# Weights of a hybrid decoder layer, laid out in DRAM by tiles

## The chip, the core and the metric

The kernel runs on one core of one Trainium2 chip. A core has a matrix engine (PE; its weight loads are shown apart as PEld), a vector engine (DVE), a scalar engine (ACT), a general engine (POOL) and a sync engine (SP) that here issues nearly all DMAs. Sixteen DMA engines move data between DRAM and the on-chip memory of 128 partitions. The metric is the device time of one execution in microseconds (us), the median of several runs. What the host does with the arrays before the launch is not part of it.

## The reference

One decoder layer on 512 tokens of width 2048, all in float32. A conditioning vector gives six modulation vectors. Then come two parallel groups of eight heads (HGRN2 and Gated DeltaNet), an output projection, and an MLP with squared ReLU.

```python
mod = c_act @ w_ada[l] + b_ada[l]                      # 2048 x 12288
sh_m, sc_m, gt_m, sh_f, sc_f, gt_f = jnp.split(mod[:, None, :], N_MOD, axis=-1)
h = rmsnorm(x, pre_mix_norm[l]) * (1.0 + sc_m) + sh_m
proj = h @ w_in[l]                                     # 2048 x 8208
o_hg = hgrn2_group(proj[..., :HG_COLS], lb_all[l], hg_norm[l])
o_gdn = gdn_group(proj[..., HG_COLS:], gdn_conv_w[l], gdn_a_log[l], gdn_dt_bias[l], gdn_norm[l])
y = jnp.concatenate([o_hg, o_gdn], axis=-1) @ w_out[l] # 2048 x 2048
x = x + gt_m * rmsnorm(y, post_mix_norm[l])
h = rmsnorm(x, pre_ffn_norm[l]) * (1.0 + sc_f) + sh_f
y = jnp.square(jax.nn.relu(h @ w_ff1[l])) @ w_ff2[l]   # 2048 x 8192, 8192 x 2048
x = x + gt_f * rmsnorm(y, post_ffn_norm[l])
```

## The kernel before

Every weight is read once; the profile counts 340 MB read from DRAM. A float32 product is made of three products of a narrower type: a matrix `a` is split into a high part `aH` and a low part `aL = a - aH`, and `mm3` adds aH·bH, aH·bL and aL·bH in PSUM.

**The weight stream.** All tiles of w_in, w_out, w_ff1 and w_ff2 go through `WeightStream` in an order fixed by `plan`. `_load` issues the DMA of a tile of 128 partitions by 1024 numbers (512 KB) into a `raw` buffer (three of them, six in the MLP), `_split` has ACT cast it to `wh` (L152) and DVE (for a few tiles of the start POOL) subtract it to `wl` (L154), and `get` hands both to PE and keeps loads up to three tiles ahead. In the MLP some w_ff2 tiles are first added or subtracted by POOL (L120).

**The start (about 0 to 200 us).** Shift and scale of the first modulation come from two segments of w_ada. `ada_slot` loads them in 128 tiles `adas` of 256 KB; ACT, DVE and POOL multiply them by the conditioning vector and add them up, PE sums over partitions, and the result modulates x block by block into `hH` and `hL`. As soon as a block of h is there, PE multiplies it with the first 32 tiles of w_in (`start_units`, heads 0 and 1). Such a tile joins two or four k-blocks of four or two column blocks of 128.

**The heads (about 200 to 1120 us).** PE runs the projections of heads 2 to 7 (`project`, tile `pj`: eight column blocks a head, each of two tiles of eight k-blocks, 96 tiles `in1`) between the recursions of the heads before. Beside them the other segments of w_ada are summed: `ada_rest` loads 192 tiles `ada` of 256 KB, 32 for each of these heads, at a pace set by `on_get`; ACT scales a tile, POOL adds it. After that come the output projection (40 tiles), the norms, and from about 1345 us the MLP (256 tiles, and 64 `ada` tiles of the last segment).

**What sets the order.** PE and SP run in the order in which the program writes their instructions, ACT too in the start; in the start and the heads the program interleaves threads by a running estimate of PE's time (`clock`) and of the loads' arrival (`on_load`). DVE and POOL, and ACT later, are ordered by the scheduler of the framework. All loads go out on SP's one queue, in order, so SP can stand at a buffer that isn't free while later loads wait behind it.

**How a tile was cut out.** In DRAM the weights have their reference layout, a row of w_in being 8208 numbers (32,832 bytes). The views below give a partition p the rows p, p+128 and so on, 128 to 512 columns each, so one partition's part of a tile is several short pieces. For w_ada, partition p takes rows 16p to 16p+15; one row is 49,152 bytes, so neighbouring partitions are 786,432 bytes apart.

```python
def w128(W, col, hf):
    return W[hf * 1024 : (hf + 1) * 1024, col : col + 128].rearrange("(k p) n -> p k n", p=P)
def wrow(W, r, nb):
    return W[r : r + 256, nb * 512 : (nb + 1) * 512].rearrange("(k p) n -> p k n", p=P)
```

Of the kernel before, what the change touches and what calls it, by code (L numbers as in the profile page):

```python
# [15 lines left out]
P = 128  # L16
# [18 lines left out]
D = 2048  # L35
# [5 lines left out]
GDN0 = 4096  # L41
C_HQ, C_HF, C_HI, C_HG = 0, 1024, 2048, 3072
C_GQ, C_GK, C_GV, C_GG, C_AB = 4096, 5120, 6144, 7168, 8192


class WeightStream:
# [41 lines left out]
    def _load(self):  # L88
        key, ap = self.loads[self.nl]
        raw = self._raw(key)  # L90
        aps = ap if isinstance(ap, list) else [ap]
        n = 1024 // len(aps)
        for j, a in enumerate(aps):
            self.nc.sync.dma_start(
                out=raw[:, j * n : (j + 1) * n].rearrange("p (k n) -> p k n", k=a.shape[1]), in_=a)
# [27 lines left out]
    def _split(self):  # L123
        i = self.ns
        e = self.plan[i]
        pool, nb = self.pool, self.bufs
        two = e[0][0] == "s2"
        if two and i not in self.raw:
            key = e[2][0]
            raw = self.raw[key]  # L130
        else:
            key = i
            raw = self.raw.pop(i)
            if two and len(e) > 3:
                key = e[2][0]
        self.uses[key] -= 1
        hn = ln = None
        if not two and len(e) > 2:
            if isinstance(self.alt, list):
                h, lo = self.alt.pop(0)  # L140
                hn = True
            else:
                pool, nb = self.alt, (0, e[2], e[2])
        if hn is None:
            tags = ("wh", "wl")
            if self.wide is not None and (two or len(e) == 2):
# [5 lines left out]
        self.cast = self.nc.scalar.copy(out=h, in_=raw).ins  # L152
        eng = self.nc.gpsimd if i in self.pool_l else self.nc.vector
        eng.tensor_tensor(out=lo, in0=raw, in1=h.bitcast(F32), op=ALU.subtract)  # L154
        ap = e[1]
        k = 2 if two else 8 if isinstance(ap, list) else ap.shape[1]
        self.hl[i] = (
            h.rearrange("p (k n) -> p k n", k=k),
            lo.rearrange("p (k n) -> p k n", k=k),
        )  # L160
        self.ns += 1
# [30 lines left out]
def hybrid_layer_kernel(  # L192
# [8 lines left out]
    PSUM = bass.MemoryType.PSUM  # L201
    xf = x[0]
    outf = out[0]
    Wi, Wo, W1, W2 = w_in[0], w_out[0], w_ff1[0], w_ff2[0]
    Wa = w_ada[0].rearrange("(p r) n -> p r n", p=P)

    const = ctx.enter_context(tc.tile_pool(name="const", bufs=1))
    big = ctx.enter_context(tc.tile_pool(name="big", bufs=1))
# [1 line left out]
    dram = ctx.enter_context(tc.tile_pool(name="dram", bufs=1, space=bass.MemoryType.DRAM))  # L210


    def w256(W, col, q):
        return W[q * 512 : (q + 1) * 512, col : col + 256].rearrange("(k p) n -> p k n", p=P)

    def wcols(W, cols, k0, nk):
        v = W[k0 * P : (k0 + nk) * P, :].rearrange("(k p) n -> p k n", p=P)
        return [v[:, :, cc : cc + P] for cc in cols]

    def w128(W, col, hf):  # L220
        return W[hf * 1024 : (hf + 1) * 1024, col : col + 128].rearrange("(k p) n -> p k n", p=P)

    def wrow(W, r, nb):
        return W[r : r + 256, nb * 512 : (nb + 1) * 512].rearrange("(k p) n -> p k n", p=P)


    G0, G1, H0, H1 = ([(k, h, cc) for cc in ccs] for k, h, ccs in (
        ("g", 0, (C_GQ, C_GK, C_GV, C_GG)), ("g", 1, (C_GQ, C_GK, C_GV, C_GG)),
        ("h", 0, (C_HF, C_HQ, C_HI, C_HG)), ("h", 1, (C_HF, C_HQ, C_HI, C_HG))))
    start_blocks = G0 + H0 + G1 + H1  # L230
    cuts = [(0, 2, 0, 16), (2, 2, 0, 16), (4, 2, 0, 8), (6, 2, 0, 8), (4, 4, 8, 16),
            (8, 4, 0, 8), (12, 4, 0, 8), (8, 4, 8, 16), (12, 4, 8, 16)]
    start_units = []
    for k0, nk, lo, hi in cuts:
        start_units += [(k0, nk, start_blocks[i : i + 8 // nk]) for i in range(lo, hi, 8 // nk)]
    NB_FF = DFF // P
    RB = 4
    NR = NB_FF // RB
    plan = []
    for i, (k0, nk, bls) in enumerate(start_units):  # L240
        plan.append((("in", i), wcols(Wi, [cc + h * P for _, h, cc in bls], k0, nk)))

    def plan_in1(col):
        for hf in range(2):
            plan.append((("in1", col, hf), w128(Wi, col, hf)))


    OUT_PAIRS = [8, 0, 10, 2, 12, 4, 14, 6]

    SLOT = dict(zip([r + i for r in OUT_PAIRS for i in (0, 1)], [i for i in range(16) if i % 4] + [0, 4, 8, 12]))  # L250

    for h in range(2, NH):
        for cc in (C_GK, C_GQ, C_GV, C_HF, C_HQ, C_HI, C_GG, C_HG):
            plan_in1(cc + h * P)
    for nbs in ((0,), (0, 1), (2,), (3,)):
        for i, r in enumerate(OUT_PAIRS):
            for nb in nbs:
                e = (("out", r, nb), wrow(Wo, r * P, nb))
                other = (nb == 3 and i >= 8 - NLAST) or (nb == 0 and len(nbs) == 2 and i > 0)
                plan.append(e + (NLAST,) if other else e)  # L260

    def plan_f2(r):
        for nb in range(4):
            for hf in range(RB // 2):
                e = (("f2", r, nb, hf), wrow(W2, r * RB * P + hf * 256, nb))
                plan.append(e + (2,) if r == NR - 1 and nb == 2 else e)


# [5 lines left out]
    def plan_s2(r, m):  # L274
        seen = set()
        for i, qa, op, qb in SEVEN:
            loads = []
            for q in (qa, qb):
                if q is not None and q not in seen:
                    seen.add(q)  # L280
                    loads.append(((r, m, q), wrow(W2, r * RB * P + (int(q[0]) - 1) * 256, m + 2 * (int(q[1]) - 1))))
# [10 lines left out]
    for kind, r, g in ff_order():  # L292
        if kind == 1:
            for q in range(4):
                plan.append((("f1", r * RB * P + g * 256, q), w256(W1, r * RB * P + g * 256, q)))
        else:
            plan_s2(r, g)
    plan_f2(NR - 1)
# [106 lines left out]
    def ada_load(alloc, col, ncol, r0, nr):  # L405
        a = alloc(f"ada{col}_{r0}")
        nc.sync.dma_start(out=a.rearrange("p (r n) -> p r n", r=nr), in_=Wa[:, r0 : r0 + nr, col : col + ncol])
        return a

    def ada_vector(a, ncol, r0, nr, acc, first):  # L410
# [138 lines left out]

    def late_loads():  # L550
        nc.sync.dma_start(out=cvr, in_=gdn_conv_w[0].rearrange("j (b n) -> (j b) n", n=P))
        nc.sync.dma_start(out=abraw, in_=Wi[:, C_AB : C_AB + 16].rearrange("(k p) n -> p k n", p=P))
# [694 lines left out]
    def ada_rest():  # L1247
# [275 lines left out]
    with ExitStack() as st:  # L1523
# [3 lines left out]
        def ada_gtf():  # L1527
# [251 lines left out]
```

## Time and profile before

| what | value |
|---|---|
| median of 3 runs | 2676.01 us (2669.79 to 2677.83) |
| the profiled execution: time, span | 2674.57 us, 2672.8 us |
| mean granted clock of PE | 0.974 |
| DMA packets | 335942, 350.66 MB, 131 GB/s on average |
| packets under 512 B, under 2 KB | 17191, 255001 |
| loads: w_in, ada, adas (median us to landing) | 10.9 (512 KB), 8.5, 5.4 (256 KB) |
| loads: w_out, w_ff (512 KB) | 3.8, 4.2 |

A view by windows has for each engine its busy time in a stretch and in brackets its instructions; then the granted clock of PE (1.00 is full speed), the mean busy share of the 16 DMA engines and the GB/s that they moved. A row of waits reads: engine, what it ran next and its line, what it had waited for, the sum in us, how often, the longest. L307 is the helper through which nearly all matmuls are recorded, so the tile's name tells them apart: `pj` projections of the heads, `pout` output projection, `pf` and `pg` the MLP.

### The profile page before, as it was taken

How to read it: one execution, taken by the hardware profiler on the slowest of the kernel's cores; microseconds unless marked ns; L12 is line 12 of the kernel's file. 1: busy time of each engine (PE TensorE's matmuls, PEld its weight loads, DVE VectorE, ACT ScalarE, POOL GpSimd, SP SyncE). 2: the span in 40 equal slices, each digit the busy share in tenths (PEclk: the TensorE clock that was granted, in tenths of full speed). 3: DMA queues.
4: the chain of work that ended last, by engine and by line, in shares of the span. 5: the costliest groups of instructions: out<-in, count | busy, mean ns of one | idle time of the engine just before them, and what ended most of it. 6: DMA issues, size and time to landing. Idle time of an engine off the chain costs nothing.

```text
span 2672.8 us, 34309 instructions
## 1 busy us (share of the span) xinstructions
PE 2497.4 (93%) x12627; PEld 2020.5 (76%) x12627; DVE 1870.6 (70%) x2709; ACT 1119.4 (42%) x1765; POOL 1036.3 (39%) x646
## 2 busy tenths in 40 slices
PE   5889999998996779999999999999999999999998
PEld 3667777787775567788778888888888888888876
DVE  7997868766764538553647668777778676777796
ACT  5543544444443324332444344444444444443333
POOL 5560344544543324000123554444544545533323
PEclk9999999999998889999999999999999999999999
DMA  9974886677889997452433334244243333332334
GB/s 289 279 192 72 133 123 138 140 151 144 146 129 100 87 117 105 91 172 95 160 115 130 111 124 136 95 135 137 96 138 129 104 130 117 106 117 86 112 103 165
DMA packets 335942, 350.66 MB, mean 131 GB/s; under 512 B 17191, under 2 KB 255001, under 8 KB 334621
## 3 DMA queue, kind: packets, MB, share of 16 engines
q1 hardware_dynamic: 335578, 348.42, 54.2%
q8 instruction: 99, 1.62, 0.2%
q14 instruction: 69, 0.57, 0.1%
q10 hardware_dynamic: 196, 0.06, 0.0%
HBM read 340.01 MB, written 8.40 MB: 130 GB/s over the span
## 4 chain that ended last, share of the span: by engine, by line
PE 62%; DVE 6%; DMA 5%; issue 2%; ACT 1%; POOL 1%; SPq 0%; DVEq 0%; POOLq 0%; ACTq 0%
PE pf L307 26%; PE pg L307 21%; PE pj L307 7%; PE pout L307 6%; DMA raw<-in_w_in_dram 4%; DVE wl L154 1%; DMA ada<-in_w_ada_dram 1%; PE pa L307 1%; DVE y L1617 0%; POOL y L1703 0%; DVE y L1607 0%; POOL aacc L427 0%; DVE x2r L1721 0%; PE p L307 0%; ACT wh L152 0%
## 5 line engine op out<-in xcount | busy, mean ns | idle before, releaser
L154 DVE TENSOR_TENSOR wl<-raw,wh 128x1024 fp32r<-128x1024 f32 x506 | 717.7, 1419 | 504.3 <-ACT wh L152 497.4
L152 ACT CAST wh<-raw 128x1024 fp32r<-128x1024 f32 x512 | 538.5, 1052 | 1016.6 <-PE pf L307 283.1
L120 POOL TENSOR_TENSOR raw<-raw,raw 128x1024 f32<-128x1024 f32 x150 | 433.4, 2905 | 409.1 <-DMA raw<-in_w_ff_dram 243.7
L307 PE MATMUL pf<-h2H,wh 128*128 128x512 f32 x1024 | 400.9, 391 | 6.6 <-ACT wh L152 6.6
L307 PE MATMUL pf<-h2H,wl 128*128 128x512 f32 x1024 | 400.9, 392 | 4.5 <-DVE wl L154 4.4
L307 PE MATMUL pf<-h2L,wh 128*128 128x512 f32 x1024 | 400.8, 391 | 0.0
L427 POOL TENSOR_TENSOR aacc<-ada,aacc 128x512 f32<-128x512 f32 x180 | 270.7, 1504 | 269.8 <-ACT ada L425 239.9
L307 PE MATMUL pj<-hH,wh 128*128 128x512 f32 x768 | 331.7, 432 | 17.0 <-ACT wh L152 17.0
L307 PE MATMUL pg<-wl,cH 128*128 128x512 f32 x840 | 327.4, 390 | 1.7 <-DVE wl L154 1.6
L307 PE MATMUL pg<-wh,cL 128*128 128x512 f32 x840 | 326.8, 389 | 0.0
L307 PE MATMUL pg<-wh,cH 128*128 128x512 f32 x840 | 326.8, 389 | 0.0
L307 PE MATMUL pj<-hH,wl 128*128 128x512 f32 x768 | 310.2, 404 | 5.3 <-DVE wl L154 5.2
L307 PE MATMUL pj<-hL,wh 128*128 128x512 f32 x768 | 309.2, 403 | 0.0
L307 PEld LDWEIGHTS pf<-h2H,wh 128*128 128x128 f32 x1024 | 193.5, 189 | 47.0 <-ACT wh L152 7.1
L307 PEld LDWEIGHTS pf<-h2H,wl 128*128 128x128 f32 x1024 | 193.5, 189 | 45.5 <-DVE wl L154 5.6
L307 PEld LDWEIGHTS pf<-h2L,wh 128*128 128x128 f32 x1024 | 193.5, 189 | 40.1
L427 POOL TENSOR_TENSOR gacc<-ada,gacc 128x512 f32<-128x512 f32 x64 | 117.4, 1834 | 268.1 <-issue 187.7
L1607 DVE TENSOR_TENSOR y<-pg,y 128x512 f32<-128x512 f32 x344 | 219.0, 681 | 0.0
L307 PEld LDWEIGHTS pj<-hH,wh 128*128 128x128 f32 x768 | 150.2, 196 | 48.0 <-ACT wh L152 18.7
L307 PEld LDWEIGHTS pg<-wl,cH 128*128 128x128 f32 x840 | 157.7, 188 | 36.3 <-DVE wl L154 3.7
L307 PEld LDWEIGHTS pj<-hH,wl 128*128 128x128 f32 x768 | 149.6, 195 | 43.9 <-DVE wl L154 10.0
L307 PEld LDWEIGHTS pg<-wh,cH 128*128 128x128 f32 x840 | 157.7, 188 | 32.8
(434 smaller groups left out, 3787.8 us busy)
## 6 DMA issues: line engine op xcount, KB each, us to landing
raw<-in_w_ff_dram SPq DMA_DIRECT2D x256, 512.0 KB, 4.2
ada<-in_w_ada_dram SPq DMA_DIRECT2D x256, 256.0 KB, 8.5
raw<-in_w_in_dram SPq DMA_DIRECT2D x96, 512.0 KB, 10.9
adas<-in_w_ada_dram SPq DMA_DIRECT2D x128, 256.0 KB, 5.4
raw<-in_w_out_dram SPq DMA_DIRECT2D x40, 512.0 KB, 3.8
raw<-in_w_in_dram SPq DMA_DIRECT2D x40, 256.0 KB, 4.7
raw<-in_w_in_dram SPq DMA_DIRECT2D x48, 128.0 KB, 5.4
xo<-in_x_dram SPq DMA_DIRECT2D x8, 512.0 KB, 9.4
```

The costliest lines, as they stand in the source:

```text
L120: self.nc.gpsimd.tensor_tensor(out=out, in0=ra, in1=rb, op=op)
L152: self.cast = self.nc.scalar.copy(out=h, in_=raw).ins
L154: eng.tensor_tensor(out=lo, in0=raw, in1=h.bitcast(F32), op=ALU.subtract)
L307: nc.tensor.matmul(ps, lhsT=lhsT, rhs=rhs, start=start, stop=stop)
L427: nc.gpsimd.tensor_tensor(out=acc, in0=a, in1=acc, op=ALU.add)
L1607: nc.vector.tensor_tensor(out=dst, in0=ps, in1=dst, op=ALU.add)
```

## The change

The host permutes w_ada, w_in, w_out, w_ff1 and w_ff2 before the launch (`by_tiles`), so that in DRAM the numbers of each tile lie together, partition after partition, and the tiles one after the other. The tiles on the chip hold what they held, at the same places. A load of a stream tile is now one DMA of one 4 KB piece per partition, and a load of a w_ada tile is one of 2 KB per partition.

| tiles | before: DMAs a tile, piece | now |
|---|---|---|
| w_in of the start, 32 | 4 (12 tiles) or 2 (20 tiles), 512 B | 1, 4 KB |
| w_in of the heads, 96 | 1, 512 B | 1, 4 KB |
| w_out 40, w_ff2 128 | 1, 2 KB | 1, 4 KB |
| w_ff1 128 | 1, 1 KB | 1, 4 KB |
| adas 128 | 1, 512 B (16 tiles) or 1 KB (112) | 1, 2 KB |
| ada 256 | 1, 2 KB, partitions 786,432 B apart | 1, 2 KB, partitions 2 KB apart |
| abraw 1 | 1, 64 B | 1, 1 KB |

The costs that the program counts for a load (`on_load(1.46)`, `on_load(0.73)`) stay, and so do the buffers.

```diff
+G0, G1, H0, H1 = ([(k, h, cc) for cc in ccs] for k, h, ccs in (
...
+def by_tiles(name, a):
...
+    if name == "w_ada":
+        w = a[0].reshape(P, KT, -1)
+        out = []
+        for g, j in SLOTS:
+            n = len(GROUPS[g]) * P
+            nr = 512 // n
+            for seg in (1, 0):
+                c0 = seg * D + GROUPS[g][0] * P
+                out.append(w[:, nr * j : nr * (j + 1), c0 : c0 + n].reshape(P, 512))
+        for seg in ADA_REST:
+            for cb in range(4):
+                for r in range(KT):
+                    out.append(w[:, r, seg * D + cb * 512 : seg * D + (cb + 1) * 512])
+        return np.stack(out)
+    if name == "w_in":
+        w = a[0].reshape(KT, P, -1).transpose(1, 0, 2)
+        out = []
+        for k0, nk, bls in START_UNITS:
+            out.append(np.concatenate([w[:, k0 : k0 + nk, cc + h * P : cc + (h + 1) * P] for _, h, cc in bls], 1))
+        for col in IN1_COLS:
+            for hf in range(2):
+                out.append(w[:, 8 * hf : 8 * (hf + 1), col : col + P])
+        return np.concatenate([t.reshape(-1) for t in out] + [w[:, :, C_AB : C_AB + 16].reshape(-1)])
+    if name == "w_ff1":
+        return a[0].reshape(4, 4, P, DFF // 256, 256).transpose(3, 0, 2, 1, 4).reshape(-1, P, 1024)
+    if name in ("w_out", "w_ff2"):
+        return a[0].reshape(-1, 2, P, 4, 512).transpose(0, 3, 2, 1, 4).reshape(-1, P, 1024)
+    return a
...
-        aps = ap if isinstance(ap, list) else [ap]
-        n = 1024 // len(aps)
-        for j, a in enumerate(aps):
-            self.nc.sync.dma_start(
-                out=raw[:, j * n : (j + 1) * n].rearrange("p (k n) -> p k n", k=a.shape[1]), in_=a)
+        self.nc.sync.dma_start(out=raw, in_=ap[0])
...
-    def w256(W, col, q):
-        return W[q * 512 : (q + 1) * 512, col : col + 256].rearrange("(k p) n -> p k n", p=P)
+    def w256(col, q):
+        return w_ff1[col // 256 * 4 + q], 4
...
     def wrow(W, r, nb):
-        return W[r : r + 256, nb * 512 : (nb + 1) * 512].rearrange("(k p) n -> p k n", p=P)
+        return W[r // 256 * 4 + nb], 2
...
-        plan.append((("in", i), wcols(Wi, [cc + h * P for _, h, cc in bls], k0, nk)))
+        plan.append((("in", i), (Wi[i], 8)))
...
-            plan.append((("in1", col, hf), w128(Wi, col, hf)))
+            plan.append((("in1", col, hf), (Wi[len(start_units) + 2 * i + hf], 8)))
...
-        nc.sync.dma_start(out=a.rearrange("p (r n) -> p r n", r=nr), in_=Wa[:, r0 : r0 + nr, col : col + ncol])
+        nc.sync.dma_start(out=a, in_=w_ada[2 * len(SLOTS) + (ADA_REST.index(seg) * 4 + cb) * KT + r])
...
-            nc.sync.dma_start(out=a.rearrange("p (r n) -> p r n", n=w), in_=Wa[:, r0 : r0 + nr, c0 : c0 + w])
+            nc.sync.dma_start(out=a, in_=w_ada[2 * i + k])
...
-        a = _np.ascontiguousarray(inputs[name])
+        a = _np.ascontiguousarray(by_tiles(name, _np.asarray(inputs[name])))
```

The instructions of PE, ACT and POOL stand in the same order as before. SP issues 56 DMAs fewer, all in the w_in tiles of the start. This is SP's program from its tenth row on, before and then now (`adas` are w_ada tiles, `xo` is x, `raw` a w_in tile; a row's last field is the shape, and x4 counts equal DMAs):

```order
L781 DMA xo<-in_x_dram 128x1024 x8
L94 DMA raw_213<-in_w_in_dram 128x2x128 x4
L761 DMA adas_0_0_218<-in_w_ada_dram 128x4x128
L761 DMA adas_0_1_220<-in_w_ada_dram 128x4x128
...
L761 DMA adas_3_1_232<-in_w_ada_dram 128x4x128
L94 DMA raw_234<-in_w_in_dram 128x2x128 x4
L94 DMA raw_239<-in_w_in_dram 128x2x128 x4
L761 DMA adas_0_0_256<-in_w_ada_dram 128x2x256
```

```order
L798 DMA xo<-in_x_dram 128x1024 x8
L140 DMA raw_213<-in_w_in_dram 128x1024
L778 DMA adas_0_0_215<-in_w_ada_dram 128x512
L778 DMA adas_0_1_217<-in_w_ada_dram 128x512
...
L778 DMA adas_3_1_229<-in_w_ada_dram 128x512
L140 DMA raw_231<-in_w_in_dram 128x1024
L140 DMA raw_233<-in_w_in_dram 128x1024
L778 DMA adas_0_0_247<-in_w_ada_dram 128x512
```

The sequence is the same; the eight DMAs of the second and third w_in tile became two.

DVE's program changes at some places of the start, where the framework's scheduler orders it. Its rows from the 69th on, before and then now (`ht` and `hL` make a block of h, `wl` is a low part of a weight tile, `asum` the running sum over w_ada tiles):

```order
L841 SCALAR_TENSOR_TENSOR ht_362<-pt_244,sc_100,R_171 128x512
L154 TENSOR_TENSOR wl_343<-raw_213,wh_342 128x1024
L414 TENSOR_SCALAR asum_1_346<-adas_0_0_218,c_99 128x128
L416 SCALAR_TENSOR_TENSOR asum_1_346<-adas_0_0_218,c_99,asum_1_346 128x128 x3
L846 SCALAR_TENSOR_TENSOR hL<-ht_362,shm,hH 128x512
L416 SCALAR_TENSOR_TENSOR asum_1_346<-adas_1_0_222,c_99,asum_1_346 128x128 x4
```

```order
L438 TENSOR_SCALAR asum_1_337<-adas_0_0_215,c_99 128x128
L858 SCALAR_TENSOR_TENSOR ht_353<-pt_235,sc_100,R_171 128x512
L199 TENSOR_TENSOR wl_334<-raw_213,wh_333 128x1024
L440 SCALAR_TENSOR_TENSOR asum_1_337<-adas_0_0_215,c_99,asum_1_337 128x128 x2
L863 SCALAR_TENSOR_TENSOR hL<-ht_353,shm,hH 128x512
L440 SCALAR_TENSOR_TENSOR asum_1_337<-adas_0_0_215,c_99,asum_1_337 128x128
L440 SCALAR_TENSOR_TENSOR asum_1_337<-adas_1_0_219,c_99,asum_1_337 128x128 x4
```

The first add over a w_ada tile moved ahead of the first block of h, and one add moved behind its low part.

More of the change, by code (lines that the diff above doesn't have):

```diff
@@ L43 @@
 C_GQ, C_GK, C_GV, C_GG, C_AB = 4096, 5120, 6144, 7168, 8192
+G0, G1, H0, H1 = ([(k, h, cc) for cc in ccs] for k, h, ccs in (
+    ("g", 0, (C_GQ, C_GK, C_GV, C_GG)), ("g", 1, (C_GQ, C_GK, C_GV, C_GG)),
+    ("h", 0, (C_HF, C_HQ, C_HI, C_HG)), ("h", 1, (C_HF, C_HQ, C_HI, C_HG))))
+START_BLOCKS = G0 + H0 + G1 + H1
+CUTS = [(0, 2, 0, 16), (2, 2, 0, 16), (4, 2, 0, 8), (6, 2, 0, 8), (4, 4, 8, 16),
+        (8, 4, 0, 8), (12, 4, 0, 8), (8, 4, 8, 16), (12, 4, 8, 16)]
+START_UNITS = [(k0, nk, START_BLOCKS[i : i + 8 // nk])
+               for k0, nk, lo, hi in CUTS for i in range(lo, hi, 8 // nk)]
+IN1_COLS = [cc + h * P for h in range(2, NH) for cc in (C_GK, C_GQ, C_GV, C_HF, C_HQ, C_HI, C_GG, C_HG)]
+GROUPS = [(0,), (1,)] + [(k, k + 1) for k in range(2, KT, 2)]
+SLOTS = [(g, j) for g, kts in enumerate(GROUPS) for j in range(4 * len(kts))]
+ADA_REST = (4, 3, 2, 5)
+def by_tiles(name, a):
+    import numpy as np
+    if name == "w_ada":
[26 more added lines that the diff above has]
+    return a
 class WeightStream:
@@ L154, in _split @@
         eng.tensor_tensor(out=lo, in0=raw, in1=h.bitcast(F32), op=ALU.subtract)
-        ap = e[1]
-        k = 2 if two else 8 if isinstance(ap, list) else ap.shape[1]
+        k = 2 if two else e[1][1]
         self.hl[i] = (
@@ L203, in hybrid_layer_kernel @@
     outf = out[0]
-    Wi, Wo, W1, W2 = w_in[0], w_out[0], w_ff1[0], w_ff2[0]
-    Wa = w_ada[0].rearrange("(p r) n -> p r n", p=P)
+    Wi = w_in[: KT * NH * P * 1024].rearrange("(i p n) -> i p n", p=P, n=1024)
+    Wab = w_in[KT * NH * P * 1024 :].rearrange("(p n) -> p n", p=P)
     const = ctx.enter_context(tc.tile_pool(name="const", bufs=1))
@@ L210, in hybrid_layer_kernel @@
     dram = ctx.enter_context(tc.tile_pool(name="dram", bufs=1, space=bass.MemoryType.DRAM))
-    def w256(W, col, q):
-        return W[q * 512 : (q + 1) * 512, col : col + 256].rearrange("(k p) n -> p k n", p=P)
[L216 to L221, printed above, removed]
-    def wrow(W, r, nb):
-        return W[r : r + 256, nb * 512 : (nb + 1) * 512].rearrange("(k p) n -> p k n", p=P)
[L227 to L235, printed above, removed]
+    def w256(col, q):
+        return w_ff1[col // 256 * 4 + q], 4
+    def wrow(W, r, nb):
+        return W[r // 256 * 4 + nb], 2
+    start_blocks, start_units = START_BLOCKS, START_UNITS
     NB_FF = DFF // P
@@ L240, in hybrid_layer_kernel @@
     for i, (k0, nk, bls) in enumerate(start_units):
-        plan.append((("in", i), wcols(Wi, [cc + h * P for _, h, cc in bls], k0, nk)))
-    def plan_in1(col):
+        plan.append((("in", i), (Wi[i], 8)))
+    for i, col in enumerate(IN1_COLS):
         for hf in range(2):
-            plan.append((("in1", col, hf), w128(Wi, col, hf)))
+            plan.append((("in1", col, hf), (Wi[len(start_units) + 2 * i + hf], 8)))
     OUT_PAIRS = [8, 0, 10, 2, 12, 4, 14, 6]
     SLOT = dict(zip([r + i for r in OUT_PAIRS for i in (0, 1)], [i for i in range(16) if i % 4] + [0, 4, 8, 12]))
-    for h in range(2, NH):
-        for cc in (C_GK, C_GQ, C_GV, C_HF, C_HQ, C_HI, C_GG, C_HG):
-            plan_in1(cc + h * P)
     for nbs in ((0,), (0, 1), (2,), (3,)):
@@ L257, in hybrid_layer_kernel @@
             for nb in nbs:
-                e = (("out", r, nb), wrow(Wo, r * P, nb))
+                e = (("out", r, nb), wrow(w_out, r * P, nb))
                 other = (nb == 3 and i >= 8 - NLAST) or (nb == 0 and len(nbs) == 2 and i > 0)
@@ L264, in plan_f2 @@
             for hf in range(RB // 2):
-                e = (("f2", r, nb, hf), wrow(W2, r * RB * P + hf * 256, nb))
+                e = (("f2", r, nb, hf), wrow(w_ff2, r * RB * P + hf * 256, nb))
                 plan.append(e + (2,) if r == NR - 1 and nb == 2 else e)
@@ L280, in plan_s2 @@
                     seen.add(q)
-                    loads.append(((r, m, q), wrow(W2, r * RB * P + (int(q[0]) - 1) * 256, m + 2 * (int(q[1]) - 1))))
+                    loads.append(((r, m, q), wrow(w_ff2, r * RB * P + (int(q[0]) - 1) * 256, m + 2 * (int(q[1]) - 1))))
             plan.append((("s2", r, m, i), loads, ((r, m, qa), op, None if qb is None else (r, m, qb))))
@@ L294, in hybrid_layer_kernel @@
             for q in range(4):
-                plan.append((("f1", r * RB * P + g * 256, q), w256(W1, r * RB * P + g * 256, q)))
+                plan.append((("f1", r * RB * P + g * 256, q), w256(r * RB * P + g * 256, q)))
         else:
@@ L403, in rsqrt_to, with ada_load @@
         nc.gpsimd.tensor_tensor(out=dst, in0=dst, in1=mhalf[:, :n], op=ALU.pow)
-    def ada_load(alloc, col, ncol, r0, nr):
-        a = alloc(f"ada{col}_{r0}")
-        nc.sync.dma_start(out=a.rearrange("p (r n) -> p r n", r=nr), in_=Wa[:, r0 : r0 + nr, col : col + ncol])
+    def ada_load(alloc, seg, cb, r):
+        a = alloc(f"ada{seg}_{cb}_{r}")
+        nc.sync.dma_start(out=a, in_=w_ada[2 * len(SLOTS) + (ADA_REST.index(seg) * 4 + cb) * KT + r])
         return a
@@ L551, in late_loads @@
         nc.sync.dma_start(out=cvr, in_=gdn_conv_w[0].rearrange("j (b n) -> (j b) n", n=P))
-        nc.sync.dma_start(out=abraw, in_=Wi[:, C_AB : C_AB + 16].rearrange("(k p) n -> p k n", p=P))
+        nc.sync.dma_start(out=abraw, in_=Wab.rearrange("p (k n) -> p k n", n=16))
         nc.sync.dma_start(out=alog, in_=gdn_a_log[0].partition_broadcast(P))
@@ L742, in on_load @@
         dma[0] = max(dma[0], clock[0]) + us
-    GROUPS = [(0,), (1,)] + [(k, k + 1) for k in range(2, KT, 2)]
-    SLOTS = [(g, j) for g, kts in enumerate(GROUPS) for j in range(4 * len(kts))]
     def ada_slot(i):
         g, j = SLOTS[i]
-        kts = GROUPS[g]
         t = []
-        nr, w = 4 // len(kts), len(kts) * P
-        for k, seg in enumerate((1, 0)):
+        for k in range(2):
             n = (2 * i + k) % (len(STAGE) + NADA)
@@ L758, in ada_slot @@
                 a = mt(STAGE[n - NADA], name, 2 if STAGE[n - NADA] in ("kT", "qT") else 1, (P, 512))
-            r0 = nr * j
-            c0 = seg * D + kts[0] * P
-            nc.sync.dma_start(out=a.rearrange("p (r n) -> p r n", n=w), in_=Wa[:, r0 : r0 + nr, c0 : c0 + w])
+            nc.sync.dma_start(out=a, in_=w_ada[2 * i + k])
             on_load(0.73)
@@ L1275, in ada_rest @@
                         lambda n: ada_pool_.tile([P, T], F32, tag="ada", bufs=LOOK + 1, name=n),
-                        s2 * D + c2_ * 512, 512, r2, 1)
+                        s2, c2_, r2)
             acc = accs_[(seg, cb)]
@@ L1534, in ada_gtf @@
                     queue.append(ada_load(lambda n: fp.tile([P, 512], F32, tag="ada", name=n, bufs=3),
-                                          5 * D + cb * 512, 512, r, 1))
+                                          5, cb, r))
                 if i >= 2:
```

## The prediction

> **What bounds the kernel now.** I read the page first: the share of each engine, then the span in slices, then the chain.
>
> ```profile
> span 2672.8 us, 34309 instructions
> PE 2497.4 (93%) x12627; PEld 2020.5 (76%) x12627; DVE 1870.6 (70%) x2709; ACT 1119.4 (42%) x1765; POOL 1036.3 (39%) x646
> PE   5889999998996779999999999999999999999998
> PEclk9999999999998889999999999999999999999999
> DMA  9974886677889997452433334244243333332334
> PE 62%; DVE 6%; DMA 5%; issue 2%; ACT 1%; POOL 1%; SPq 0%; DVEq 0%; POOLq 0%; ACTq 0%
> ```
>
> PE is busy 93% of the span, so everything that is not PE can give back at most 2672.8 − 2497.4 = 175 us, and a little more where PE runs at a lower clock. A slice is 66.8 us. DMA is full in two places: the first slices (0 to 200 us) and slices 13 to 16 (about 800 to 1000 us). At both PE falls below 9, and in the second its clock does too. Next, the busy time of all engines by stage.
>
> ```profile
> core 0: us, PE busy (x) PEld busy (x) DVE busy (x) ACT busy (x) POOL busy (x), PEclk, DMA share, GB/s
> 0.00:30.00 30.00, 6.83 (x22) 3.74 (x22) 17.96 (x75) 15.28 (x30) 16.43 (x66) 1.00 0.99 299
> 30.00:170.00 140.00, 115.97 (x587) 88.85 (x587) 131.91 (x186) 75.88 (x152) 78.29 (x52) 0.94 0.98 272
> 275.00:600.00 325.00, 307.49 (x2079) 247.67 (x2078) 242.77 (x504) 159.31 (x349) 146.14 (x116) 0.97 0.74 139
> 600.00:800.00 200.00, 187.63 (x1181) 148.54 (x1180) 139.68 (x253) 91.26 (x174) 97.32 (x75) 0.99 0.81 139
> 800.00:1000.00 200.00, 144.75 (x748) 111.04 (x747) 86.09 (x164) 61.14 (x120) 55.70 (x45) 0.85 0.95 101
> 1040.00:1080.00 40.00, 39.36 (x220) 31.81 (x219) 30.16 (x67) 10.27 (x14) 4.99 (x5) 1.00 0.64 81
> ...
> 1600.00:2000.00 400.00, 400.00 (x1766) 331.33 (x1765) 306.13 (x319) 171.08 (x196) 186.59 (x76) 1.00 0.37 122
> ...
> 2616.00:2628.00 12.00, 11.97 (x53) 9.25 (x52) 10.64 (x15) 6.32 (x11) 0.97 (x1) 1.00 1.00 408
> ```
>
> From 800 to 1000 the DMA engines are busy 95% of the time and move only 101 GB/s. From 2616 to 2628, where the tail reads `x2d` in rows of 8 KB (beside one broadcast vector), a full DMA moves 408 GB/s. So the transfers of the heads stage are slow, not many. Who waits for them there:
>
> ```profile
> ACT wh L152 <- DMA raw<-in_w_in_dram: 108.9, 14, 10.5
> ```
>
> ACT's cast of a weight tile, the first step of every split into high and low parts, stands 108.9 us for w_in tiles in these 200 us. Between 1600 and 2000 PE is busy all 400 us, so faster loads of w_ff1 and w_ff2 have nothing to give there.
>
> **The heads stage, the main term.** The same loads take twice as long from one stretch to the next (issues by line, KB each, median us to landing; first 600 to 800, then 800 to 1000):
>
> ```profile
> DMA packets 34228, 27.86 MB, mean 139 GB/s; under 512 B 1280, under 2 KB 27174, under 8 KB 34214
> ada<-in_w_ada_dram SPq DMA_DIRECT2D x57, 256.0 KB, 10.2
> raw<-in_w_in_dram SPq DMA_DIRECT2D x26, 512.0 KB, 11.1
> ```
> ```profile
> DMA packets 24654, 20.16 MB, mean 101 GB/s; under 512 B 956, under 2 KB 19506, under 8 KB 24644
> ada<-in_w_ada_dram SPq DMA_DIRECT2D x39, 256.0 KB, 17.6
> raw<-in_w_in_dram SPq DMA_DIRECT2D x18, 512.0 KB, 22.7
> ```
>
> Kinds and sizes are the same, yet a packet costs 0.95 × 200 × 16 / 24654 = 123 ns of an engine in the second stretch and 0.81 × 200 × 16 / 34228 = 76 ns in the first. What differs is which addresses are read: another head's columns and another segment of w_ada. I read this as a cost of the strided pattern (128 rows of w_in 32,832 bytes apart, 128 groups of w_ada rows 786,432 bytes apart). The change replaces it with one closed block per tile. The nearest rows for long pieces are these:
>
> ```profile
> raw<-in_w_ff_dram SPq DMA_DIRECT2D x256, 512.0 KB, 4.2
> raw<-in_w_out_dram SPq DMA_DIRECT2D x40, 512.0 KB, 3.8
> ```
>
> Half of the w_ff loads and all of w_out read 2 KB pieces and land in about 4 us, against 22.7. A head needs 16 w_in tiles of 512 KB and 32 w_ada tiles of 256 KB (192 tiles over six heads), 16.8 MB. At 101 GB/s that takes 166 us, and at 408 GB/s 41 us. What PE alone needs comes from its projection matmuls (tile `pj`, the same stretches):
>
> ```profile
> 600.00:800.00 200.00, 160.20 (x634) 115.17 (x633) 3.41 (x5) 10.12 (x17) 0.99 0.81 139
> 800.00:1000.00 200.00, 121.60 (x413) 84.44 (x412) 2.05 (x3) 6.44 (x11) 0.85 0.95 101
> ```
>
> From 600 to 800 PE does 634 of them, 3.17 a microsecond, at 94% busy. The 413 from 800 to 1000 would take 413 / 3.17 = 130 us at that pace: **−70 us**. It includes the clock, 0.85 beside 0.99. Next in line once the loads are early is PE itself (188 of 200 us at that pace), with DVE at 70%. The lower bound of the saving is nothing, if the slow stretch stays. With the stall gone, its floor is the slower pace of the earlier heads:
>
> ```profile
> 275.00:300.00 25.00, 6.58 (x27) 4.99 (x27) 0.00 (x0) 0.00 (x0) 1.00 0.76 130
> 275.00:600.00 325.00, 231.54 (x874) 160.34 (x875) 4.08 (x6) 15.52 (x26) 0.97 0.74 139
> ```
>
> The projections only begin in the first 25 us; without these, 847 in 300 us are 2.82 a microsecond, and 413 / 2.82 = 146 us saves 54. Between 275 and 800 itself PE idles for 18 of 325 and 12 of 200 us. Its largest wait from 275 to 600 is for a step of the heads' recursions, not for a load, so I give only 3 us there (0 to 8).
>
> ```profile
> PE p L307 <- DVE S L1129: 9.2, 4, 2.6
> ```
>
> **The start.** All of 0 to 200 us runs at full DMA too, but DVE is busy 131.9 of 140 us from 30 to 170, and its waits in the first 205 us name no DMA at all. Its two largest, and ACT's two waits for loads:
>
> ```profile
> DVE ht L841 <- PE pt L318: 6.3, 6, 2.6
> DVE c L531 <- ACT cth L530: 4.8, 1, 4.8
> ACT wh L152 <- DMA raw<-in_w_in_dram: 5.1, 2, 4.4
> ACT junkx L609 <- DMA xo<-in_x_dram: 3.0, 3, 2.6
> ```
>
> So faster loads meet an engine with 140 − 132 = 8 us to spare. Two loads early on do gate it. x queues behind the first eight `adas` tiles (2 MB in 512-byte pieces) and costs ACT 2.6 us. And the second w_in tiles are issued late, eight DMAs in 4.90 us of SP, which is two after the change:
>
> ```profile
> 26.86 4.90 SPq L94 DMA_DIRECT2D raw<-in_w_in_dram  x8
> ...
> 33.49 1.05 ACT L152 CAST wh<-raw 128x1024 fp32r<-128x1024 f32 x1 [4.41 <-DMA raw<-in_w_in_dram]
> ```
>
> The sum of both, 2.6 + 4.4, is **−7 us**. The low end is 0, if DVE's adds swallow both waits. The high end is 16: DVE's 8 idle us of the middle and half of its first 12, plus 2. SP drops 56 of its DMAs (48 of 128 KB and 40 of 256 KB become 32 of 512 KB); that is in the 4.4, and later SP only waits for buffers. DVE's program order changes by a few places in the start, with equal work. I cost that at 0, between −2 and 2, by the size of one such displaced step.
>
> **The rest.** w_out and w_ff: after 1160 ACT waits 20.7 us for w_out tiles in ten pieces, but PE names no wait for that cast there; its one long wait, 6.6 us, is for the cast of a first w_ff1 tile.
>
> ```profile
> ACT wh L152 <- DMA raw<-in_w_out_dram: 20.7, 10, 4.0
> PE pf L307 <- ACT wh L152: 6.6, 1, 6.6
> ```
>
> From 1000 to the end I give −5 us (0 to 12): a fourth of these 20.7 reaching PE through later splits, at most PE's 6.6 with it. Cover: in the MLP a load lands in 4.2 us while PE has a queue of work; PE at 400 of 400 is what hides the edit.
>
> **Sum.** 70 + 7 + 3 + 5 = 85 us off the profiled execution, 2674.57 us (its span 2672.8 and 1.8 around it): 2589.6. The median of the three runs, 2676.01, is 1.4 above, so **2590 us** in round numbers.
>
> The Trainium skill, "DMA: Bandwidth & Descriptors", Specifications, puts the smallest transfer for line rate at 512 B, which speaks against this change, since hardly a piece is shorter. The trace disagrees in one row and agrees in another: 512-byte pieces alone gave 81 GB/s at a share of 0.64 from 1040 to 1080, while pieces of 512 B and 1 KB gave 272 at 0.98 in the start.
>
> **Rivals.** (a) Part of the slow stretch is not the pattern: say `ada` tiles or the memory behind them stay slow at half the loss. Then 35 of the 70 us go: 2625. For it: nothing in the trace separates the w_in and w_ada loads, which share one queue. Against: both are laid out anew.
> (b) Piece length and order do not set the rate, so the loads stay as slow as they are: the main term and the load-bound parts are zero, 2676 less a few us in SP's issue, 2673. For it: packets of nearly the same size cost 76 and 123 ns. Against: 408 GB/s for closed 1 MB blocks. It is also the case in which the change does not do what it says. By the Trainium skill's 512 B rule (the same section) the result would be this one.
> (c) Slower: a tile as one closed block puts all 16 engines on neighbouring addresses at the same time, and if that is slow, every head runs at the rate of 800 to 1000. It decides once the heads get less than PE's pace needs, 16.8 MB in 120 us, 140 GB/s. At 101 GB/s each of the four heads before 800 would take 166 instead of about 125 us, +164: 2840. For it: 101 GB/s exists in this kernel. Against: x2r reads closed blocks at 408.
>
> **How the numbers follow.** Forecast 0.83, (a) 0.08, (b) 0.06, (c) 0.03. The forecast's own bounds: 54 + 0 at the little end gives 2676 − 54 = 2622, and 77 + 16 + 8 + 12 = 113 at the other gives 2563 (77 with PE at 100 instead of 94%: 3.17 / 0.94 = 3.37 a microsecond). The range reaches to (a) with a little for its start: **2562 to 2630**. Leaving out (b), (c) and the edges of the forecast is no more than 2 in 10. A measurement of this kernel tells about 0.3% (8 us) from no change. Faster by more than that: forecast and (a), 0.91. Within: (b), 0.06. Slower: (c), 0.03.
>
> **What would show it.** Right: `raw<-in_w_in` landing near 4 us with 4 KB packets, DMA share below 0.6 from 600 on, no ACT wait for raw above a few us in head 6, PE clock 1.0 there, `pj` at 3.1 or more a microsecond to the end of the heads, and DVE still above 90% busy until about 170. Wrong: DMA above 0.9 in the heads, or the start shorter by more than 16 us, which would say that DVE had been waiting behind loads in a way its waits do not name.

## The result, and the profile after

The changed kernel takes 2602.9 us (median of 4 runs, 2601.19 to 2604.4) against 2675.41 us before (median of 4, 2669.79 to 2677.83). The ratio is 0.9732, with a 95% interval of 0.9715 to 0.9749: 72.5 us less, where 85 were forecast. The profiled execution took 2601.19 us with a span of 2599.4, at a mean granted clock of 0.982 (before 0.974).

The page of the changed kernel: span and engines, three of the rows in 40 slices (now 65 us each), the packets, and the first row of the chain.

```profile
span 2599.4 us, 34113 instructions
PE 2476.1 (95%) x12627; PEld 2008.6 (77%) x12627; DVE 1876.1 (72%) x2709; ACT 1119.0 (43%) x1765; POOL 1034.3 (40%) x646
...
PE   5889999998999899999899999999999999999998
...
PEclk9999999999999999999899999999999999999999
DMA  9762434444544432435323333333324334233234
...
DMA packets 127300, 350.64 MB, mean 135 GB/s; under 512 B 14247, under 2 KB 18713, under 8 KB 125981
...
PE 66%; DVE 6%; POOL 1%; ACT 1%; issue 1%; DMA 1%; SPq 0%; DVEq 0%; ACTq 0%; POOLq 0%
```

The hole in PE and in its clock of slices 13 to 15 (about 800 to 1000 us) is gone, and DMA's part of the chain of waits fell from 5% to 1%. The busy time of the engines by stretch, with the same columns as before:

```profile
30.00:170.00 140.00, 115.56 (x586) 88.62 (x584) 130.71 (x185) 75.54 (x152) 77.62 (x52) 0.91 0.79 265
...
600.00:800.00 200.00, 187.69 (x1183) 148.64 (x1182) 139.30 (x253) 90.18 (x172) 96.43 (x75) 0.99 0.49 153
800.00:1000.00 200.00, 190.52 (x1125) 154.05 (x1123) 148.74 (x273) 91.02 (x180) 87.61 (x69) 0.97 0.39 128
```

From 800 to 1000 PE is busy 190.52 us instead of 144.75, with the DMA engines at 39% instead of 95%. From 30 to 170, though, PE and DVE did almost the same work in the same time as before (586 matmuls and 587, 185 DVE instructions and 186), although the share of DMA fell from 0.98 to 0.79. The loads of 800 to 1000 (median us to landing in the last field), and ACT's longest waits there:

```profile
ada<-in_w_ada_dram SPq DMA_DIRECT2D x41, 256.0 KB, 3.4
raw<-in_w_in_dram SPq DMA_DIRECT2D x27, 512.0 KB, 3.4
```
```profile
ACT wh L197 <- PE pj L331: 48.8, 15, 11.4
ACT thvT L497 <- DVE zvT L493: 9.5, 2, 5.3
```

A w_in tile lands in 3.4 us instead of 22.7, and the wait of 108.9 us for one is gone. ACT's longest wait is now for PE, which I read as a buffer that PE has yet to free: PE, busy 95% of the stretch, sets the pace of the heads, as forecast.

Where the 73.4 us between the two profiled executions went can be read from four instructions that end a stage in both: the copy of the decay terms that ends the start (`gT`), the last matmul over the sums of w_ada (`pca`), the first load of `wpost`, which SP issues once the heads are done with, and the last store of the output. Each row has the shortest, median and longest duration in ns, then the first and the last start in us. Before, then now:

```profile
L729 DVE COPY gT<-pgt x1: 278/278/278, 216.3 to 216.3; 32x128 f32<-32x128 f32 x1
L307 PE MATMUL pca<-ones,aacc x128: 222/222/271, 368.2 to 758.5; 128*64 128x64 f32 x128
L1392 SPq DMA_DIRECT2D wpost<-in_post_mix_norm_dram x4: 328/376/461, 1106.7 to 1122.7; - x4
L1723 SPq DMA_DIRECT2D out_dram<-x2r x10: 332/332/403, 2649.1 to 2669.2; - x10
```
```profile
L753 DVE COPY gT<-pgt x1: 278/278/278, 216.5 to 216.5; 32x128 f32<-32x128 f32 x1
L331 PE MATMUL pca<-ones,aacc x128: 222/222/270, 366.8 to 757.1; 128*64 128x64 f32 x128
L1409 SPq DMA_DIRECT2D wpost<-in_post_mix_norm_dram x4: 327/375/426, 1034.0 to 1050.1; - x4
L1740 SPq DMA_DIRECT2D out_dram<-x2r x10: 332/332/398, 2575.7 to 2595.8; - x10
```

| stage | before, us | now, us | saved | forecast |
|---|---|---|---|---|
| start, to `gT` | 216.3 | 216.5 | −0.2 | 7 |
| `gT` to the last `pca` | 542.2 | 540.6 | 1.6 | 3 |
| last `pca` to the first `wpost` | 348.2 | 276.9 | 71.3 | 70 |
| `wpost` to the last store | 1562.5 | 1561.8 | 0.7 | 5 |

The forecast's stretches (275 to 800, 800 to 1000, 1000 to the end) lie near these stages and not exactly on them. Practically all of it comes from one stage, and the other transfers, which are laid out anew just as thoroughly, give nothing that this measurement can tell. Three questions follow: which of the loads it was, what about the old layout was slow, and why the start gave nothing.

### The profile page after: what moved, and what is told of

It reads as the page before. It is cut to its first block, busy times and chain, and to the rows that moved or that the text cites. A ratio compares the mean times of both kernels' runs of the same rounds, so it can differ in the third digit from the quotient of the medians.

```text
span 2599.4 us, 34113 instructions
## 1 busy us (share of the span) xinstructions
PE 2476.1 (95%) x12627; PEld 2008.6 (77%) x12627; DVE 1876.1 (72%) x2709; ACT 1119.0 (43%) x1765; POOL 1034.3 (40%) x646
## 4 chain that ended last, share of the span: by engine, by line
PE 66%; DVE 6%; POOL 1%; ACT 1%; issue 1%; DMA 1%; SPq 0%; DVEq 0%; ACTq 0%; POOLq 0%
PE pf L331 26%; PE pg L331 21%; PE pj L331 9%; PE pout L331 7%; DVE wl L199 1%; PE pa L331 1%; DMA ada<-in_w_ada_dram 1%; DVE y L1634 0%; POOL y L1720 0%; DVE y L1624 0%; DVE uc L1034 0%; POOL aacc L451 0%; DVE utmp L1032 0%; DVE x2r L1738 0%; PE p L331 0%
## 5 line engine op out<-in xcount | busy, mean ns | idle before, releaser
L165 POOL TENSOR_TENSOR raw<-raw,raw 128x1024 f32<-128x1024 f32 x150 | 439.9, 2948 | 401.6 <-DMA raw<-in_w_ff_dram 154.0
L331 PE MATMUL pj<-hH,wh 128*128 128x512 f32 x768 | 325.3, 424 | 0.0
L331 PE MATMUL pj<-hL,wh 128*128 128x512 f32 x768 | 304.0, 396 | 0.0
L451 POOL TENSOR_TENSOR gacc<-ada,gacc 128x512 f32<-128x512 f32 x64 | 108.5, 1695 | 277.9 <-ACT ada L449 277.9
L331 PEld LDWEIGHTS pg<-wh,cL 128*128 128x128 f32 x840 | 157.7, 188 | 32.6
```

The costliest lines, as they stand in the source:

```text
L165: self.nc.gpsimd.tensor_tensor(out=out, in0=ra, in1=rb, op=op)
L331: nc.tensor.matmul(ps, lhsT=lhsT, rhs=rhs, start=start, stop=stop)
L451: nc.gpsimd.tensor_tensor(out=acc, in0=a, in1=acc, op=ALU.add)
```

## The experiments

My theory was that of the prediction: the heads were slow because w_in and w_ada were read in short, scattered pieces. Its rivals: only one of the two matters; the piece length doesn't matter but the addresses do; and, for the start, that DVE and not the loads set its end. Each kernel below the first row ran once, beside one run of the kernel before on the same chip; the first row has medians of four. The runs of the kernel before lie within 0.3% (8 us) of each other, so a difference of a few us is read from the traces, not from these times.

| kernel | us | before beside it, us | w_in tile of the heads lands after, us | `ada` tile, us |
|---|---|---|---|---|
| the change | 2602.9 | 2675.41 | 3.4 (all 128) | 3.5 |
| w_in of the heads alone | 2605.25 | 2670.84 | 3.5 | 3.7 |
| `ada` of the heads alone | 2672.05 | 2670.84 | 10.3 | 8.3 |
| start alone | 2668.06 | 2670.84 | 11.2 | 8.3 |
| closed block of 512 B pieces | 2605.07 | 2670.84 | 4.1 | 3.9 |
| heads 3 and 6 exchanged | 2661.09 | 2674.82 | 11.1 | 8.1 |
| rows of 33,280 B | 2603.72 | 2674.82 | 4.1 | 3.9 |
| rows of 36,928 B | 2605.64 | 2677.44 | 3.9 | 3.8 |
| 33,280 B, 64 B off | 2604.36 | 2677.44 | 3.9 | 3.9 |
| rows of 32,768 B | 2603.5 | 2677.44 | 4.2 | 3.9 |

### Which loads it was

The first kernel is the one of before, with only the 96 w_in tiles of the heads laid out tile by tile (a second array beside the old one).

```diff
-            plan.append((("in1", col, hf), w128(Wi, col, hf)))
+            plan.append((("in1", col, hf), (Wt[len(start_units) + 2 * IN1_COLS.index(col) + hf], 8)))
```

> Kernel before, with only the 96 w_in tiles of the heads in tile order; the w_ada tiles keep their rows 49,152 bytes apart. If the strided w_in tiles alone made the slow stretch: about 2603 us, w_in tiles landing near 4 us and no wait of ACT above a few us in head 6. If the w_ada tiles made it: about 2675 us, with ACT's waits for w_in near 100 us. If both share it: 2620 to 2655.

The second has only the 256 `ada` tiles laid out.

```diff
-in_=Wa[:, r0 : r0 + nr, col : col + ncol])
+in_=At[2 * len(SLOTS) + (ADA_REST.index(col // D) * 4 + col % D // 512) * KT + r0]
```

> Kernel before, with only the 256 ada tiles (heads and MLP) in tile order; w_in keeps its layout. The mirror of the other run: if w_in alone made the slow stretch about 2675 us, if w_ada alone about 2603 us, if both share it 2620 to 2655.

The stretch from 800 to 1000 of the first and then of the second kernel, with the loads of each (the first's over the whole execution, the second's in that stretch):

```profile
800.00:1000.00 200.00, 190.89 (x1125) 154.50 (x1124) 148.37 (x276) 91.33 (x182) 90.53 (x71) 0.97 0.40 129
```
```profile
ada<-in_w_ada_dram SPq DMA_DIRECT2D x256, 256.0 KB, 3.7
raw<-in_w_in_t_dram SPq DMA_DIRECT2D x96, 512.0 KB, 3.5
```
```profile
800.00:1000.00 200.00, 149.31 (x775) 114.05 (x774) 87.14 (x168) 60.95 (x120) 56.45 (x46) 0.85 0.95 102
```
```profile
ada<-in_w_ada_t_dram SPq DMA_DIRECT2D x39, 256.0 KB, 18.1
raw<-in_w_in_dram SPq DMA_DIRECT2D x18, 512.0 KB, 22.6
```

With w_in alone the hole is filled (65.6 us less than the run beside it). With `ada` alone nothing changes, and an `ada` tile that is now one closed block still takes 18.1 us. With w_in laid out, the `ada` tiles land in 3.7 us from their old places, 786,432 bytes apart. So they were not slow themselves; they go out on one queue, in between w_in tiles. The loss was w_in's alone.

### The start alone

The third kernel has only the 128 `adas` and the 32 w_in tiles of the start laid out.

```diff
-        plan.append((("in", i), wcols(Wi, [cc + h * P for _, h, cc in bls], k0, nk)))
+        plan.append((("in", i), (Wt[i], 8)))
...
-in_=Wa[:, r0 : r0 + nr, c0 : c0 + w])
+in_=At[2 * i + k])
```

> Kernel before, with only the start's loads in tile order (128 adas tiles, 32 w_in tiles). If DVE, POOL and ACT bound the start and swallow what the loads give: about 2675 us, the copy gT that ends the decay terms at 216 us as before. If the start gives the 7 us that were forecast, and something else in the full change took them back: 2668 us, gT at 209 us.

```profile
L786 DVE COPY gT<-pgt x1: 278/278/278, 215.4 to 215.4; 32x128 f32<-32x128 f32 x1
```

The start ends 0.9 us earlier than before, and the hole from 800 on stays (PE busy 147.05 of 200 us). The time of 2668.06 us happens to be the one that the second expectation named, but the kernel before took only 2670.84 us beside it, and 2.8 us is within the spread of the runs; `gT` at 215.4 instead of 209 decides for the first. So the start is worth about 1 us here, and 0 in the full change.

### What of w_in was slow: pieces, columns or the distance of rows

The next kernel lays out both as the change does, but inside a w_in tile's closed 512 KB block each partition still reads eight pieces of 512 B, 64 KB apart.

```diff
-                out.append(w[:, 8 * hf : 8 * (hf + 1), col : col + P])
+                out.append(w[:, 8 * hf : 8 * (hf + 1), col : col + P].transpose(1, 0, 2))
```

> Kernel before, with the 96 w_in tiles of the heads each in one closed block of 512 KB, but in the order of the reference inside it, so that a partition still takes eight pieces of 512 bytes, 64 KB apart; the ada tiles in tile order. If it is the distance over DRAM that made the loads slow: about 2603 us and landings of w_in below 6 us. If it is the length of the pieces: waits of ACT for w_in come back, landings above 8 us and more than 2620 us.

```profile
DMA packets 335942, 350.66 MB, mean 135 GB/s; under 512 B 17191, under 2 KB 255001, under 8 KB 334621
ada<-in_w_ada_t_dram SPq DMA_DIRECT2D x256, 256.0 KB, 3.9
raw<-in_w_in_t_dram SPq DMA_DIRECT2D x96, 512.0 KB, 4.1
```

The packets are those of before to the last one, 335942 with the same counts by size, and the time is that of the change within the spread of the runs. Longer pieces are not what it was.

The next kernel keeps the old layout and exchanges the columns of heads 3 and 6 of w_in in DRAM. The kernel reads each where it now lies, so the program computes the same in the same order.

```diff
-            plan.append((("in1", col, hf), w128(Wi, col, hf)))
+            h = col % 1024 // P
+            at = col + ({3: 6, 6: 3}.get(h, h) - h) * P
+            plan.append((("in1", col, hf), w128(Wi, at, hf)))
```

> Kernel before, with the w_in columns of heads 3 and 6 exchanged in DRAM and read where they now lie; order, shapes and pieces stay. If the slow loads belong to the columns (which bytes of a row are read): head 3 (about 430 to 560 us) becomes slow, its w_in tiles landing near 20 us instead of 7, and head 6 fast, total 2665 to 2690. If they belong to the time or to what else runs beside head 6: landings of 20 us stay at 800 to 1000, total 2675.

The stretch from 400 to 600 before, and then 400 to 600 and 800 to 1000 with the columns exchanged; behind them the w_in loads from 400 to 560, before and then exchanged:

```profile
400.00:600.00 200.00, 190.07 (x1295) 153.25 (x1294) 150.28 (x309) 95.36 (x212) 92.45 (x73) 0.98 0.68 144
```
```profile
400.00:600.00 200.00, 151.40 (x909) 117.19 (x907) 109.43 (x234) 65.81 (x138) 64.56 (x53) 0.89 0.95 93
...
800.00:1000.00 200.00, 187.90 (x1195) 149.62 (x1195) 140.09 (x246) 91.49 (x176) 97.09 (x74) 0.98 0.76 154
```
```profile
raw<-in_w_in_dram SPq DMA_DIRECT2D x19, 512.0 KB, 7.9
```
```profile
raw<-in_w_in_dram SPq DMA_DIRECT2D x14, 512.0 KB, 24.5
```

The hole moved to 400 to 600 with the columns. It belongs to the bytes of a row that are read, not to that place in the program or to what runs beside it. The total, 2661.09 us, missed both expectations: it is 13.7 us less than the run beside it, below the 2665 to 2690 named. So what the slow columns cost does depend somewhat on where they are read; why is not shown.

The next kernel is that of before, with 448 bytes of zeros behind each row of w_in: rows 33,280 instead of 32,832 bytes apart. Nothing else changes.

```diff
         a = _np.ascontiguousarray(inputs[name])
+        if name == "w_in":
+            a = _np.concatenate([a, _np.zeros(a.shape[:-1] + (112,), a.dtype)], -1)
```

> Kernel before, with rows of w_in lengthened from 32,832 to 33,280 bytes (65 x 512), so that all 512-byte pieces start at a multiple of 512 bytes; still eight scattered pieces per partition. If it is the uneven start of the pieces that is slow: landings of w_in tiles near 4 us and about 2603 us. If it is the scatter over rows: landings of 8 us and more, above 2640 us.

From 800 to 1000, the stretch and its packets and loads:

```profile
800.00:1000.00 200.00, 189.91 (x1137) 153.58 (x1137) 149.18 (x275) 90.94 (x180) 87.34 (x70) 0.98 0.43 129
```
```profile
DMA packets 34749, 25.86 MB, mean 129 GB/s; under 512 B 1140, under 2 KB 29226, under 8 KB 34734
...
raw<-in_w_in_dram SPq DMA_DIRECT2D x26, 512.0 KB, 4.1
ada<-in_w_ada_dram SPq DMA_DIRECT2D x43, 256.0 KB, 3.7
```

This is the whole gain, as far as these runs can tell (71.1 us), from 448 bytes a row, with every piece as short and as scattered as before. A packet now costs 0.43 × 200 × 16 / 34749 = 40 ns of an engine, where the prediction counted 123.

Is it that pieces start at multiples of 512 B now? In rows of 32,832 bytes (32,768 + 64) they start at any multiple of 64. Two kernels keep uneven starts: one pads to 36,928 bytes (9 × 4,096 + 64), the other has rows of 33,280 bytes and 64 bytes of zeros ahead of each row. A third takes the 16 decay columns into an array of their own, so that rows are exactly 32,768 bytes.

```diff
+            a = _np.concatenate([a, _np.zeros(a.shape[:-1] + (1024,), a.dtype)], -1)
```

> Kernel before, with rows of w_in lengthened from 32,832 to 36,928 bytes (9 x 4096 + 64): each row starts 64 bytes further round a block of 512 than the one before, as in the kernel before, but rows are no longer close to a power of two apart. If the uneven start of the pieces is slow: about as before, 2660 to 2680, landings of w_in tiles of 8 us and more. If it is the distance of the rows (addresses of 128 partitions meeting in the same part of the memory): about 2603 us, landings near 4 us.

```diff
+            a = _np.concatenate([_np.zeros(a.shape[:-1] + (16,), a.dtype), a, _np.zeros(a.shape[:-1] + (96,), a.dtype)], -1)
```

> Kernel before with rows of 33,280 bytes as in pitch_33280, which came to 2603.72 us, but with 64 bytes ahead of each row's numbers, so that every piece of 512 bytes starts 64 bytes past a multiple of 512. If the uneven start is slow: landings of 8 us and more, 2640 to 2680 us. If the distance of the rows is: 2603 us and landings near 4 us, as without the 64 bytes.

```diff
+            a = _np.concatenate([a[0][:, :C_AB].reshape(-1), a[0][:, C_AB:].reshape(-1)])
```

> Kernel before, with the sixteen decay columns taken out of w_in, so that its rows are 32,768 bytes (a power of two) and all pieces start at a multiple of 512 bytes. If only the start of the pieces matters: 2603 us and landings near 4 us. If the distance of the rows matters, a power of two should be the worst of all: landings above 10 us from 240 us on, 2700 us or more.

The w_in loads of the heads over the whole of each execution, in that order:

```profile
raw<-in_w_in_dram SPq DMA_DIRECT2D x96, 512.0 KB, 3.9
```
```profile
raw<-in_w_in_dram SPq DMA_DIRECT2D x96, 512.0 KB, 3.9
```
```profile
raw<-in_w_in_dram SPq DMA_DIRECT2D x96, 512.0 KB, 4.2
```

All three are fast. So uneven starts alone are not the cause, and a power of two, where I had expected the worst, is not slow either. Of the four row distances tried, only 32,832 bytes is slow. It is also the only one that is close to a power of two and has uneven starts, so that it may take both together; no run separates that. Nor did any run move the array as a whole in DRAM with its rows left as they were.

### Why the start gave nothing

In the next two runs the kernel before and the changed one leave out 92 of the 160 products over `adas` that DVE adds up in the start. All loads stay; the sums over w_ada are then incomplete, so only the times of these two are of use.

```diff
-        for r in range(nr):
+        for r in range(1):
```

> Kernel before; it leaves out DVE's products of the start beyond the first of each adas tile (92 of 160, so the scale of the first modulation and the first block's shift are partial sums). If the loads held the start as much as DVE, gT stays near 216 us, since the loads run at a share of 0.98: 205 us or more. If DVE alone held it, gT comes as early as in the twin with the new layout.

> The changed kernel with the same 92 products left out. If DVE bound its start: gT at 160 to 190 us instead of 216.5, and the total shorter by the same. If ACT, POOL or the order of the program bound it: gT within 5 us of 216.5.

The old layout first, then the new:

```profile
30.00:170.00 140.00, 123.04 (x652) 95.45 (x651) 108.70 (x140) 82.69 (x165) 85.70 (x59) 0.95 1.01 287
```
```profile
L729 DVE COPY gT<-pgt x1: 279/279/279, 200.3 to 200.3; 32x128 f32<-32x128 f32 x1
```
```profile
30.00:170.00 140.00, 126.31 (x677) 98.38 (x677) 111.89 (x142) 85.63 (x170) 93.15 (x62) 0.98 0.81 284
```
```profile
L753 DVE COPY gT<-pgt x1: 279/279/279, 194.3 to 194.3; 32x128 f32<-32x128 f32 x1
```

With less for DVE to do the start ends 16.0 us earlier in the old layout and 22.2 in the new, and the totals follow: 2657.12 us against 2674.82 beside it, and 2579.03 against the change's 2602.9. DVE set the start's end. The old layout came out between its two expectations, with DVE in front and the loads 6 us behind it. The new one came out 4 us later than the 160 to 190 us that I had expected of it; POOL, at 93.15 of 140 us, or the order of the work may be next, which no run tested. Only now do the two layouts part, by 200.3 − 194.3 = 6.0 us, with the old one at a DMA share of 1.01. That is about the size of the forecast's 7 us, though nothing shows that it is made of the same two waits.

The last kernel is the changed one with the program's own costs for a load set to what the new loads suggest, so that the start is written out for earlier arrivals.

```diff
-on_load(1.46)
+on_load(1.25)
...
-on_load(0.73)
+on_load(0.62)
```

> The changed kernel with the costs that the program counts for a load lowered in the ratio of the new to the old speed (1.46 to 1.25, 0.73 to 0.62), which moves PE's, ACT's and SP's order in the start. If DVE bounds the start whatever the order: within 4 us of 2602.9. If the order still waits for loads that are long there: 5 to 10 us less.

```profile
30.00:170.00 140.00, 101.49 (x496) 77.37 (x496) 124.55 (x174) 71.49 (x149) 76.56 (x51) 0.89 0.73 248
```
```profile
PE pc L331 <- DVE asum L440: 15.1, 6, 4.8
```

It takes 2626.1 us, 23 more than the change, and both expectations missed. The second of these rows is PE's largest wait from 30 to 320 us (4.5 us in the changed kernel): I read it so that PE's fixed order now asks for the sums over w_ada before DVE has them. PE did 496 matmuls in the 140 us instead of 586, and the start's blocks moved behind: the last of its first group of products (tile `accg`) starts at 245.2 us instead of 219.8. No version that computes the whole layer came out ahead of the change.

## Why the prediction was right, and where it was not

**The heads, 70 us.** Right in place and size: 71.3 us between the last `pca` and the first `wpost`. The working holds too. With the loads early PE is next in line, and `pj` runs at 643 matmuls in 200 us, 3.2 a microsecond where 3.17 were assumed. The clock came to 0.97, not to the 1.0 named as a sign.

```profile
800.00:1000.00 200.00, 164.37 (x643) 119.41 (x643) 2.72 (x4) 11.13 (x19) 0.97 0.39 128
```

The cause in it was half wrong. "I read this as a cost of the strided pattern" named w_in and w_ada together; w_ada was innocent, and of w_in it was neither the pieces nor their scatter, but rows 32,832 bytes apart. The forecast's number did not depend on this, since the change removes the row distance along with the strides. Rival (b) had its premise right, that piece length does not set the rate, and its conclusion wrong, that the loads then stay slow.

The prediction held the row from 1040 to 1080 (81 GB/s from 512-byte pieces) against the Trainium skill's 512 B rule ("DMA: Bandwidth & Descriptors", Specifications). That fell: the row too comes from w_in tiles with rows 32,832 bytes apart, while 512-byte pieces at other row distances land as a 512 KB tile in 3.9 to 4.2 us, against 3.4 to 3.5 for 4 KB pieces. So these runs speak for the rule more than against it. Nearer to the case is what the Trainium skill says on the same page, in "Latency and other measured facts": there, large powers of two as the distance between partitions (2 to 8 MiB) are slow, and 4 KiB more than 4 MiB cures it while 192 B more does not. No run here has a distance of that size. Here the slow distance is 64 B above a far smaller power of two, 448 B more cured it as fully as 4,096, and the power of two itself was fast. The remedies that the Trainium skill names there, padding the row or laying tiles out closed, both worked.

**The start, 7 us.** Wrong: 0, at the low end that the prediction named, "if DVE's adds swallow both waits". The step that failed is the sum 2.6 + 4.4: it took two waits of ACT as if ACT's time reached the end of the stage. Only one of them shrank as reckoned, ACT's wait for w_in, from 5.1 to 1.5 us in all. The wait for x stayed at 3.0 us in all: its first part fell from 2.6 to 1.4, but later pieces of x now hold ACT up instead. ACT's two waits in the changed kernel:

```profile
ACT junkx L633 <- DMA xo<-in_x_dram: 3.0, 5, 1.4
ACT wh L197 <- DMA raw<-in_w_in_dram: 1.5, 1, 1.5
```

And what ACT gained did not reach the end, because DVE has as much to do as before (130.71 us of 140, still above 90%); the two layouts part only when its work is cut. The prediction also had "All of 0 to 200 us runs at full DMA", which is a misreading: from 170 to 200 the share was 0.62. It had the slow stretch in slices 13 to 16, where the rows show 13 to 15. Neither enters the sum.

**275 to 800, 3 us, and 1000 to the end, 5 us.** 1.6 (from `gT` on) and 0.7, both inside their ranges. A fourth of ACT's 20.7 us for w_out was too much to let through, and 14.5 us of that wait are still there in the changed kernel. In the MLP PE is busy 400 of 400 us in both, as said. The three terms other than the heads were 15 us in the forecast and 2.1 measured, which is the whole miss of some 12 us.

**What stays open.** What in the memory makes 32,832 bytes slow, and why one head's columns take two to three times as long as the others (before, a median of 22.7 us to landing from 800 to 1000, against 11.1 from 600 to 800 and 7.9 from 400 to 560). The runs show that it goes with the row distance and the place in the row. They do not show whether closeness to a power of two, the uneven starts and the array's place in DRAM have to come together.

## What to carry to other kernels

When the same kind of load, at the same size, takes twice as long from one stretch to the next, look at its addresses, and try a few hundred bytes of padding a row before laying out all weights anew: here one array and 448 bytes gave what the permutation of five arrays gave. A load that lands late may only be standing in a queue behind a slow one: lay out one array at a time to see which it is. A DMA share of 0.98 does not say that a stage waits for loads; ask which engine has no time to spare. Here the waits of that engine, DVE, named no load.

## What the runs showed of the hardware that was not expected

- A tile of 1,024 pieces of 512 B, from rows 32,832 bytes apart, took a median of 10.9 us to land, and 22.7 us in the stretch of the slowest head; from rows 32,768, 33,280 or 36,928 bytes apart it took 3.9 to 4.2 us.
- A distance of 786,432 bytes between the partitions of a tile, in 2 KB pieces, cost next to nothing: 3.7 us from there against 3.5 from a closed block.
- Eight times longer pieces bought little once the distance was right: 4.1 against 3.5 us for 512 KB.
